# Windowed attention inside an F32 two-mixer layer: values held stationary, turned probabilities moving, and identity products at the start

## The chip, the core and the metric

The kernel runs on one core of one Trainium2 chip. Its time is the device time of one execution in microseconds (us). TensorE (PE, with its weight loads PEld), VectorE (DVE), ScalarE (ACT), GpSimd (POOL) and SyncE (SP, which issues the transfers) each work through an instruction list of their own. PE reads its stationary operand into the array with a weight load and then streams the moving operand through it; products land in PSUM, which has eight banks of 128 partitions by 512 F32 values.

## What is computed

Two layers follow one another on 512 rows of 1,024 features. The first has neighbourhood attention beside a state-space mixer and a gated FFN. The second, in which most of the change lies, is windowed attention with 16 query heads, 4 key/value heads of 64 features, a bias by relative position and one sink logit per head, and then a SwiGLU FFN.

```python
h = rmsnorm(x, mix_norm_pre) * (1.0 + sc1) + sh1
q, k, v = split(h @ w_qkv)                       # 16, 4, 4 heads of 64
# blocks of 128 queries see the block before, their own and the one behind
logits = q k^T * 64**-0.5 + bias[bucket(rel)]    # masked to |rel| <= 128
p = softmax(concat([logits, sink]))[..., :-1]
out = (p @ v).reshape(S, 16 * 64) @ w_o
x = x + g1 * rmsnorm(out, mix_norm_post)
```

## The kernel before

Weights arrive by DMA in raw F32 chunks (`wr`); ACT rounds a chunk to F32R (`wh`, L152) and DVE takes the rest (`wl`, L153), so that a product is three F32R products: high by high, high by low, low by high (`mm3`, L89 to L91). Activations are kept in the same two parts (`hh`, `hl`), with features on partitions.

The kernel is written as a program of tiles. Which instruction stands where on an engine is settled when the program is built; while it runs, each engine keeps to its list and waits for what an instruction needs. Buffers come from rings (`slots`, some with one or two buffers), and PSUM banks are handed out by roles (`psum(...)`); in the heads there are two banks for the wide products, three for scores (`PS`), two for transposes (`PT`) and one for the attention output (`PO`).

In the attention of mixer 2, `wide(...)` makes ten tiles of queries and keys, [128 features x 512 rows] each, with 24 products of 512 columns a tile. From the fourth tile on, two heads (a pair) run beside the next tile's products, so that six pairs lie beside tiles and the last two pairs (heads 12 to 15) behind them. `head(h)` takes four query blocks n. Each block has w = 256 or 384 keys, and for each:

1. two score products of w columns (L1048, L1049) into a PSUM bank;
2. DVE adds the bias and takes the row minimum (L1051, with a read of the accumulator behind it), ACT takes the exponential and the row sums (L1053);
3. PE transposes the 128x128 squares of the probabilities (L1056), two or three of them;
4. a copy brings them to SBUF, on DVE for odd blocks (L1059) and on ACT for even ones (L1061);
5. PE multiplies with the turned probabilities as the stationary operand and 64 columns of `v` moving, in F32 (L1064). There are 10 such products a head, and each is two entries in the trace: 320 entries for 16 heads.

Behind the four blocks come the sink's exponential (L1065), the sum, the reciprocal (L1066, L1067) and the scaling into `on` (L1068), with rows on partitions. `turn_o(a)` (L1073 to L1081) transposes eight finished heads back to features on partitions, in 16 transposes with a high part on ACT and a low part on DVE for each of four row blocks: once beside the last heads (for heads 0 to 7), once behind head 15 (for heads 8 to 15). The output projection then runs through `nat_out` (L825, L829) with `oT` as its stationary operand.

At the start, x is loaded, normalised on DVE (L307) and transposed on PE (L338); a row of modulation values is made by products with 32 columns of `cs32` (`gemv2`, L318) and brought to columns (`columns`, copy L324, transposes L326, L327 to L332); `features` (L340 to L342) makes `hh` and `hl`, which the first products (L89) need.

Of the kernel before, what the change touches and what calls it, by code (L numbers as in the profile page):

```python
# [11 lines left out]
F32 = mybir.dt.float32  # L12
# [26 lines left out]
def tile_hybrid_then_windowed_gqa(ctx, tc, A, out, dbg=None):  # L39
# [152 lines left out]
    make_identity(nc, ident)  # L192
    onesr = CT(128, F32R, base="one")
# [806 lines left out]
    Q, VV, BI, PS_ = slots(ap_, "q", 16), slots(ap_, "v", 2), slots(ap_, "bi", 2), slots(ap_, "sc", 3)  # L1000
    PP = slots(ap_, "pp", 3)
# [8 lines left out]
    on = [ap_.tile([128, 4, 512], F32, tag=f"on{a}", name=f"on{a}") for a in range(2)]  # L1010
# [20 lines left out]
    po2 = []  # L1031

    def head(h):
        kvh = h // 4
        bt = BI(n=384)
        nc.sync.dma_start(out=bt, in_=A["bias2"][h])
        if h % 2 == 0:
            po2.append(PO())
        po, st = po2[-1][:, 256 * (h % 2):256 * (h % 2) + 256], SS(n=20)
        for n in range(4):  # L1040
            j0, j1 = max(0, n - 1), min(4, n + 2)
            nk = j1 - j0
            w = 128 * nk
# [6 lines left out]
            sc = PS_(n=384)  # L1050
            V.tensor_tensor_reduce(sc[:, :w], s[:, :w], bt[:, b0:b0 + w], -1.0, nsink[:, h:h + 1],  # L1051
                                   ALU.add, ALU.min, st[:, n:n + 1])
            act(sc[:, :w], sc[:, :w], AF.Exp, scale=-1.0, bias=st[:, n:n + 1], accum_out=st[:, 4 + n:5 + n])  # L1053
            pt = PT()
# [10 lines left out]
        act(st[:, 8:12], st[:, 0:4], AF.Exp, bias=sk[:, h:h + 1])  # L1065
        V.tensor_add(st[:, 12:16], st[:, 4:8], st[:, 8:12])  # L1066
        V.reciprocal(st[:, 16:20], st[:, 12:16])  # L1067
        V.tensor_tensor(on[h // 8][:, :, 64 * (h % 8):64 * (h % 8) + 64], hd(po, 4),  # L1068
                        st[:, 16:20, None].to_broadcast([128, 4, 64]), op=ALU.mult)

    oT = {}

    def turn_o(a):  # L1073
        for tb in range(4):
            p = PT()
            for f in range(4):
                tr(p[:, 128 * f:128 * f + 128], on[a][:, tb, 128 * f:128 * f + 128], ident)
            hi, lo = Q(F32R), Q(F32R)
            act(hi, p, AF.Copy)
            V.tensor_sub(lo, p, hi)  # L1080
            oT[tb, a] = hi, lo  # L1081

    def use_and_attend(i, p):
# [3 lines left out]
        if i == 3:  # L1087
            ws = [load_w(Wq, 4 * a, 4, [(1280, 256)]) for a in range(2)]
            for t2 in range(2):
# [6 lines left out]
                t = VV()  # L1096
                V.tensor_copy(t, pv)
                vv.extend([t[:, 0:256], t[:, 256:512]])
# [4 lines left out]
        if i == 9:  # L1103
            turn_o(0)
# [169 lines left out]
```

## Time and profile before

| | |
|---|---|
| time, three runs | 1347.13, 1351.51, 1354.16 us (median 1351.51) |
| profiled execution | 1350.22 us, span 1348.4 us, mean granted TensorE clock 0.995 |
| busy, share of the span | PE 97%, PEld 81%, DVE 59%, ACT 43%, POOL 7% |
| chain that ended last | PE 79%, DVE 10%, DMA 4%, ACT 3%, POOL 2% |
| L1064, values times probabilities | 320 entries, PE busy 43.1 us, PEld busy 41.3 us |

The busy shares are means over stages with different limits, so that the stages have to be read one by one. In a window's row the figures are its bounds, its length, the busy time of PE, PEld, DVE, ACT and POOL with the number of instructions, the granted clock (1.00 is 2.4 GHz), the DMA engines' share and GB/s. In a timeline's row they are the start, the duration, the line and the operation; starts that follow one another closer than the durations tell what an instruction costs, since neighbours overlap. In a row of lines they are the number of instructions, their busy time, the mean duration in ns and the engine's idle time ahead of them with what ended it.

### The profile page before, as it was taken

Reading aid. Unit: us, or ns where it says so; the run is one execution under the profiler, and the core shown is the slowest. Engines: PE = TensorE matmul, PEld = TensorE weight load, DVE = VectorE, ACT = ScalarE, POOL = GpSimd, SP = SyncE. Lnnn points to the kernel's source line nnn. Section 1 sums busy time; section 2 is a strip of 40 time slices with the busy share of each in tenths; the row PEclk is TensorE's granted clock in tenths of the full one; section 3 lists DMA queues with packets and bytes.
Section 4 is the critical chain, followed back from the end, with each engine's and each line's share of the span. In section 5 each row is a group of like instructions: output and inputs, shape, how many; then the busy total and the mean of one; then the engine's idle time right before and its main releaser. Section 6 shows DMA issues by size and latency. Waiting matters only on the chain.

```text
span 1348.4 us, 18115 instructions
## 1 busy us (share of the span) xinstructions
PE 1302.4 (97%) x6927; PEld 1092.6 (81%) x6927; DVE 790.4 (59%) x1443; ACT 581.3 (43%) x1040; POOL 93.0 (7%) x101
## 2 busy tenths in 40 slices
PE   6999999998999999999999999999999999999997
PEld 3687778997879888888788798888798888888886
DVE  5786996666685766675953666666553222325323
ACT  2546446765555333333433555565552222224221
POOL 0013560000000000000000310000000000000000
PEclk9999999999999999999999999999999999999999
DMA  8763131043553654665654112212133332223321
GB/s 284 262 204 109 47 103 55 22 130 124 195 196 109 219 170 158 218 213 168 232 168 143 61 60 80 62 57 63 57 95 94 98 104 96 94 94 96 106 79 63
DMA packets 53238, 168.14 MB, mean 125 GB/s; under 512 B 6048, under 2 KB 11424, under 8 KB 53152
## 3 DMA queue, kind: packets, MB, share of 16 engines
q1 hardware_dynamic: 53152, 166.99, 38.3%
q8 instruction: 55, 0.90, 0.3%
q14 instruction: 31, 0.25, 0.1%
HBM read 164.87 MB, written 2.10 MB: 124 GB/s over the span
## 4 chain that ended last, share of the span: by engine, by line
PE 79%; DVE 10%; DMA 4%; ACT 3%; POOL 2%; issue 2%; SPq 0%; POOLq 0%; DVEq 0%; ACTq 0%
PE bank L825 19%; PE bank L89 16%; PE bank L90 16%; PE bank L91 15%; PE bank L1064 3%; PE bank L765 2%; DMA ada<-in_ada_w 2%; PE bank L1056 1%; DVE acc L226 1%; PE bank L759 1%; DVE wl L153 1%; PE bank L1048 1%; POOL sm L207 1%; PE bank L1049 1%; DMA wr<-in_w_in_tiles 1%
## 5 line engine op out<-in xcount | busy, mean ns | idle before, releaser
L90 PE MATMUL bank<-hl,wh 128*128 128x512 f32 (+1 forms) x1040 | 389.0, 374 | 2.1 <-DVE hl L917 1.5
L89 PE MATMUL bank<-hh,wh 128*128 128x512 f32 (+1 forms) x1040 | 388.5, 376 | 0.8 <-DVE b L383 0.7
L91 PE MATMUL bank<-hh,wl 128*128 128x512 f32 (+1 forms) x1040 | 388.8, 374 | 0.0
L152 ACT ACTIVATE wh<-wr 128x1024 fp32r<-128x1024 f32 x173 | 182.1, 1059 | 393.1 <-PE bank L90 286.7
L153 DVE TENSOR_TENSOR wl<-wr,wh 128x1024 fp32r<-128x1024 f32 x173 | 212.2, 1228 | 196.2 <-ACT wh L152 196.0
L90 PEld LDWEIGHTS bank<-hl,wh 128*128 128x128 f32 x1040 | 197.2, 190 | 34.8 <-DVE hl L917 2.9
L89 PEld LDWEIGHTS bank<-hh,wh 128*128 128x128 f32 x1040 | 196.4, 190 | 34.1 <-DVE b L383 1.0
L91 PEld LDWEIGHTS bank<-hh,wl 128*128 128x128 f32 x1040 | 197.1, 190 | 31.4
L825 PE MATMUL bank<-wh,act 128*128 128x512 f32 x544 | 146.2, 389 | 0.0
L825 PEld LDWEIGHTS bank<-wh,act 128*128 128x128 f32 x544 | 102.1, 188 | 21.5 <-issue 0.3
L226 DVE SCALAR_TENSOR_TENSOR acc<-ada,cs,acc 128x1024 f32<-128x1024 f32 x70 | 91.0, 1299 | 22.0 <-DMA ada<-in_ada_w 21.7
L972 DVE TENSOR_TENSOR act<-bank,act 128x512 f32<-128x512 f32 x44 | 30.4, 690 | 92.6 <-PE bank L91 92.5
L825 PE MATMUL bank<-wl,act 128*128 128x512 f32 x272 | 84.0, 389 | 0.0
L207 POOL TENSOR_TENSOR sm<-sm,mh 128x1 f32<-128x1 f32 x28 | 17.3, 618 | 657.6 <-DVE sm L206 657.6
L825 PEld LDWEIGHTS bank<-wl,act 128*128 128x128 f32 x272 | 51.0, 188 | 10.6
L825 PE MATMUL bank<-act,act 128*128 128x512 f32 x240 | 56.8, 397 | 0.0
L825 PEld LDWEIGHTS bank<-act,act 128*128 128x128 f32 x240 | 46.0, 193 | 9.7
L1064 PEld LDWEIGHTS bank<-v,pp 128*128 128x128 f32 x320 | 41.3, 191 | 5.5 <-ACT pp L1061 2.3
L1064 PE MATMUL bank<-v,pp 128*128 128x64 f32 x320 | 43.1, 271 | 0.1
L982 DVE TENSOR_TENSOR act<-act,act 128x512 fp32r<-128x512 f32 x44 | 29.5, 686 | 20.7 <-PE bank L825 20.0
L1053 ACT ACTIVATE sc<-sc,ss 128x256 f32<-128x256 f32 (+1 forms) x64 | 35.6, 557 | 12.8 <-DVE ss L1051 9.0
L1051 DVE CUSTOM_DVE_ANT_0 sc<-bank,bi,nsink 128x256 f32<-128x256 f32 (+1 forms) x64 | 33.7, 543 | 10.0 <-PE bank L1049 8.2
(324 smaller groups left out, 1885.9 us busy)
## 6 DMA issues: line engine op xcount, KB each, us to landing
ada<-in_ada_w SPq DMA_DIRECT2D x80, 512.0 KB, 4.4
wr<-in_ffn_w_up_tiles SPq DMA_DIRECT2D x44, 512.0 KB, 4.4
wr<-in_ffn_w_in_tiles SPq DMA_DIRECT2D x44, 512.0 KB, 3.6
wr<-in_ffn_w_down SPq DMA_DIRECT2D x22, 512.0 KB, 4.5
wr<-in_ffn_w_out SPq DMA_DIRECT2D x22, 512.0 KB, 3.4
wr<-in_w_in_tiles SPq DMA_DIRECT2D x19, 512.0 KB, 4.4
wr<-in_att_w_qkv_tiles SPq DMA_DIRECT2D x10, 512.0 KB, 3.7
ada<-in_ada SPq DMA_DIRECT2D x8, 512.0 KB, 5.2
```

Of the source, the lines that this page charges most:

```text
L89: mm(o, lh, rh, start=start, stop=False)
L90: mm(o, lh, rl, start=False, stop=False)
L91: mm(o, ll, rh, start=False, stop=stop)
L152: act(hi[:, :n], raw[:, :n], AF.Copy)
L153: V.tensor_sub(lo[:, :n], raw[:, :n], hi[:, :n])
L207: GP.tensor_tensor(ms[:, 1:2], ms[:, 0:1], mhalf, op=ALU.pow)
L226: V.scalar_tensor_tensor(acc, raw, csil[:, ci + k:ci + k + 1], acc, op0=ALU.mult, op1=ALU.add)
L825: mm(ps[tb][a], l, r[a], start=start and l is lh and r is w[0], stop=stop and l is ll)
L972: V.tensor_mul(actT[ft], p, actT[ft])
L1051: V.tensor_tensor_reduce(sc[:, :w], s[:, :w], bt[:, b0:b0 + w], -1.0, nsink[:, h:h + 1], ALU.add, ALU.min, st[:, n:n + 1])
L1053: act(sc[:, :w], sc[:, :w], AF.Exp, scale=-1.0, bias=st[:, n:n + 1], accum_out=st[:, 4 + n:5 + n])
L1064: mm(o, P[:, 128 * i:128 * i + 128], vv[j0 + i][:, 64 * kvh:64 * kvh + 64], start=i == 0, stop=i == nk - 1)
```

## The change

Two parts of the kernel are touched.

In the attention, operands are exchanged: `v` (now kept as a high and a low half beside one another, 128 columns for each kv head) is the stationary operand, and the turned probabilities move through it with 256 or 384 columns. For that they are kept in two F32R parts, `ph` (ACT) and `pl` (DVE), one pair of tiles for a head. A head has eight products, all into the one `PO` bank, with the product of the high half of `v` on one half of the partitions and that of the low half on the other; ACT copies one half (L1086) and DVE adds the other (L1087). Sums and reciprocals are taken apart: the reciprocals of a pair are spread over 64 columns each (L1094), transposed (L1097), and multiplied on (L1098). The pair's output is then already turned, so `turn_o` goes; its two parts (L1100, L1101) are the `oT` of one k. The score buffers are a ring of seven in place of three. In the program's text the scores of all four blocks, with what DVE and ACT do to them, now come ahead of the first transpose.

At the start, eight F32 products of the identity with a broadcast column of itself (512 columns) go into a bank that is free; nothing reads them.

```diff
+    idle = PO()
+    for _ in range(8):
+        mm(idle, ident, ident[:, 0:1].to_broadcast([128, 512]), start=True, stop=True)
...
-    Q, VV, BI, PS_ = slots(ap_, "q", 16), slots(ap_, "v", 2), slots(ap_, "bi", 2), slots(ap_, "sc", 3)
-    PP = slots(ap_, "pp", 3)
+    Q, VV, BI = slots(ap_, "q", 16), slots(ap_, "v", 2), slots(ap_, "bi", 2)
+    sc_ring = itertools.cycle([XN] * 4 + [XT] * 3)
...
+    op, sums, RS, RX = [], [], slots(ap_, "rs", 2), slots(ap_, "rx", 1)
     def head(h):
...
+            scs.append(sc)
+        act(st[:, 8:12], st[:, 0:4], AF.Exp, bias=sk[:, h:h + 1])
+        V.tensor_add(rs[:, 4 * s2:4 * s2 + 4], st[:, 4:8], st[:, 8:12])
+
+        ph, pl = (ap_.tile([128, 4, 512], F32R, tag=f"on{a}", name=nm("p")).rearrange("p a b -> p (a b)")
+                  for a in range(2))
+        for n, (j0, j1) in enumerate(spans):
+            nk, sc = j1 - j0, scs[n]
             pt = PT()
             for i in range(nk):
                 tr(pt[:, 128 * i:128 * i + 128], sc[:, 128 * i:128 * i + 128], ident)
-            P = PP(n=384)
-            if n % 2:
-                V.tensor_copy(P[:, :w], pt[:, :w])
-            else:
-                act(P[:, :w], pt[:, :w], AF.Copy)
-            o = po[:, 64 * n:64 * n + 64]
-            for i in range(nk):
-                mm(o, P[:, 128 * i:128 * i + 128], vv[j0 + i][:, 64 * kvh:64 * kvh + 64], start=i == 0, stop=i == nk - 1)
...
+            at = 256 * j0 + 128 * n + 128
+            hi, lo = (t[:, at:at + 256 * nk].rearrange("p (k n) -> p k n", k=nk)[:, :, 0:128] for t in (ph, pl))
+            src = pt[:, :128 * nk].rearrange("p (k n) -> p k n", k=nk)
+            act(hi, src, AF.Copy)
+            V.tensor_sub(lo, src, hi)
+        po = PO()
+        for j in range(4):
+            n0, n1 = max(0, j - 1), min(4, j + 2)
+            a = 384 * j + 128 * (n0 - j + 1)
+            for part in (ph, pl):
+                mm(po[:, 128 * n0:128 * n1], vv[j][:, 128 * kvh:128 * kvh + 128], part[:, a:a + 128 * (n1 - n0)],
+                   start=j == 0 and part is ph, stop=j == 3 and part is pl, skip_group_check=True)
...
+        act(o[own, :], po[other, :], AF.Copy)
+        V.tensor_add(o[own, :], po[own, :], o[own, :])
+        if s2:
+
+            V.reciprocal(rs, rs)
+            pr = PT()
+            rx = RX()
+            for s in range(2):
+                V.tensor_copy(rx.rearrange("p (n s d) -> p n s d", n=4, s=2)[:, :, s, :],
+                              rs[:, 4 * s:4 * s + 4, None].to_broadcast([128, 4, 64]))
+            for n in range(4):
+                tr(pr[:, 128 * n:128 * n + 128], rx[:, 128 * n:128 * n + 128], ident)
+            V.tensor_mul(o, o, pr)
+            hi, lo = Q(F32R), Q(F32R)
+            act(hi, o, AF.Copy)
+            V.tensor_sub(lo, o, hi)
+            oT[h // 2] = hi, lo
...
-                t = VV()
-                V.tensor_copy(t, pv)
...
+                act(tv[:, :, 0, :], hd(pv, 8), AF.Copy)
+                V.tensor_sub(tv[:, :, 1, :], hd(pv, 8), tv[:, :, 0, :])
...
-        if i == 9:
-            turn_o(0)
...
-    turn_o(1)
     def lhs_o(tb, k):
-        hi, lo = oT[tb, k // 4]
-        c = slice(128 * (k % 4), 128 * (k % 4) + 128)
+        hi, lo = oT[k]
+        c = slice(128 * tb, 128 * tb + 128)
```

On PE the change shows most beside a wide tile. Before, this stands there in one pair (`pp` holds turned probabilities, `sc` the ones not yet turned, `q` queries and keys, `hh`, `hl`, `wh`, `wl` the wide tile):

```order
L1064 MATMUL bank_7801<-v_7090,pp_7812 128x64 x2
L1056 MATMUL bank_7837<-id_107,sc_7834 128x128 x3
L89 MATMUL bank_7932<-hh_6457,wh_7928 128x512
L90 MATMUL bank_7932<-hl_6458,wh_7928 128x512
L91 MATMUL bank_7932<-hh_6457,wl_7929 128x512
L89 MATMUL bank_7932<-hh_6457,wh_7928 128x512
L1064 MATMUL bank_7801<-v_7090,pp_7826 128x64 x2
L1064 MATMUL bank_7801<-v_7141,pp_7826 128x64
L1064 MATMUL bank_7801<-v_7090,pp_7841 128x64
L1064 MATMUL bank_7801<-v_7141,pp_7841 128x64 x2
L1056 MATMUL bank_7852<-id_107,sc_7849 128x128 x2
```

After the change, in the same stage (`p` holds one part of the turned probabilities, `xn` and `xt` take the place of `sc`, `rx` holds the spread reciprocals):

```order
L1080 MATMUL bank_7814<-p_7791,v_7097 128x256
L1080 MATMUL bank_7814<-p_7790,v_7097 128x384
L1053 MATMUL bank_7898<-q_6960,q_7689 128x256
L1054 MATMUL bank_7898<-q_6963,q_7689 128x256
L91 MATMUL bank_8026<-hh_6466,wl_8023 128x512
L89 MATMUL bank_8026<-hh_6466,wh_8022 128x512
L1080 MATMUL bank_7814<-p_7791,v_7097 128x384
L1080 MATMUL bank_7814<-p_7790,v_7149 128x384
L1080 MATMUL bank_7814<-p_7791,v_7149 128x384
L1080 MATMUL bank_7814<-p_7790,v_7149 128x256
L1080 MATMUL bank_7814<-p_7791,v_7149 128x256
L1097 MATMUL bank_7826<-id_107,rx_7827 128x128 x4
```

Single products of 64 columns, each with a weight load of its own from `pp`, have become products of 256 or 384 columns on two weights of `v`, and four more transposes of `rx` stand in a pair.

On DVE, before, in the same pair as above, one head's four score blocks with the work between them:

```order
L1051 ISA sc_7806,ss_7802<-bank_7803,bi_7799,nsink_6741 128x256
L1051 ISA ss_7802 128x1
L1051 ISA sc_7819,ss_7802<-bank_7816,bi_7799,nsink_6741 128x384
L1051 ISA ss_7802 128x1
L1051 ISA sc_7834,ss_7802<-bank_7831,bi_7799,nsink_6741 128x384
L1051 ISA ss_7802 128x1
L1027 SCALAR_TENSOR_TENSOR q_7793<-bank_7768,q_7793 64x512
L1051 ISA sc_7849,ss_7802<-bank_7846,bi_7799,nsink_6741 128x256
L1051 ISA ss_7802 128x1
L153 TENSOR_TENSOR wl_8479<-wr_8090,wh_8478 128x1024
L1027 SCALAR_TENSOR_TENSOR q_7796<-bank_7768,q_7796 64x512
L1059 COPY pp_7826<-bank_7822 128x384
```

On DVE after the change, across the end of one head and the start of the next pair's first:

```order
L1074 TENSOR_TENSOR p_7791<-bank_7803,p_7790 128x3x128
L1074 TENSOR_TENSOR p_7791<-bank_7809,p_7790 128x2x128
L1094 COPY rx_7827<-rs_7698 128x4x64 x2
L1056 ISA xt_7889,ss_7878<-bank_7886,bi_7876,nsink_6750 128x384
L1056 ISA ss_7878 128x1
L1056 ISA xt_7895,ss_7878<-bank_7892,bi_7876,nsink_6750 128x384
L1056 ISA ss_7878 128x1
L1087 TENSOR_TENSOR tm_7758<-bank_7814,tm_7758 64x512
L1056 ISA xn_7901,ss_7878<-bank_7898,bi_7876,nsink_6750 128x256
L1056 ISA ss_7878 128x1
L1098 TENSOR_TENSOR tm_7758<-tm_7758,bank_7826 128x512
L1074 TENSOR_TENSOR p_7907<-bank_7908,p_7906 128x2x128
```

The copies of `pp` on every second block are gone; a subtraction that reads the bank and ACT's part (L1074) stands there for every block, and the two copies into `rx`, the addition, the multiplication and the low part of the output (which follows this piece) have come in.

On PE at the start, before, the transposes of x (`b`) stand first, and half of them ahead of the products on the modulation weights (`ada`, `n`):

```order
L338 MATMUL bank_179<-id_107,b_77 128x128
L338 MATMUL bank_179<-id_107,b_81 128x128
L338 MATMUL bank_229<-id_107,b_77 128x128
L338 MATMUL bank_229<-id_107,b_81 128x128
L318 MATMUL bank_158<-ada_93,sel_120 32x256 x4
L318 MATMUL bank_158<-n_95,sel_120 32x256 x2
L318 MATMUL bank_158<-n_97,sel_120 32x256 x2
L338 MATMUL bank_179<-id_107,b_85 128x128
L338 MATMUL bank_179<-id_107,b_89 128x128
L338 MATMUL bank_229<-id_107,b_85 128x128
L338 MATMUL bank_229<-id_107,b_89 128x128
L326 MATMUL bank_158<-id_107,t_167 128x128 x2
```

After the change:

```order
L196 MATMUL bank_112<-id_107 128x512 x8
L322 MATMUL bank_167<-ada_93,sel_129 32x256 x4
L322 MATMUL bank_167<-n_95,sel_129 32x256 x2
L322 MATMUL bank_167<-n_97,sel_129 32x256 x2
L342 MATMUL bank_188<-id_107,b_77 128x128
L342 MATMUL bank_188<-id_107,b_81 128x128
L342 MATMUL bank_188<-id_107,b_85 128x128
L342 MATMUL bank_188<-id_107,b_89 128x128
L322 MATMUL bank_209<-ada_101,sel_129 32x256
L330 MATMUL bank_167<-id_107,t_176 128x128 x2
```

The identity products stand ahead of everything, and the first set of modulation products ahead of the first transposes of x.

## Rows read from the trace of the kernel before

**Rows 1.** Windows: six pairs beside tiles; the sixth alone; heads 12 to 15.

```profile
816.60:905.69 89.09, 89.09 (x604) 78.19 (x602) 58.78 (x174) 54.66 (x150) 0.00 (x0) 1.00 0.23 69
890.88:905.69 14.81, 14.81 (x102) 13.00 (x100) 9.72 (x29) 9.06 (x26) 0.00 (x0) 1.00 0.20 64
905.69:936.20 30.51, 29.70 (x214) 25.66 (x213) 21.63 (x64) 20.75 (x56) 0.00 (x0) 1.00 0.16 49
```

**Rows 2.** Timeline of PE inside the sixth pair.

```profile
895.91 0.48 PE L89 MATMUL bank<-hh,wh 128*128 128x512 f32 x1
896.22 0.40 PE L90 MATMUL bank<-hl,wh 128*128 128x512 f32 x1
896.46 0.40 PE L91 MATMUL bank<-hh,wl 128*128 128x512 f32 x1
...
896.92 1.45 PE L1064 MATMUL bank<-v,pp 128*128 128x64 f32 x12
898.21 0.39 PE L1056 MATMUL bank<-id,sc 128*128 128x128 f32 x2
898.35 0.36 PE L1048 MATMUL bank<-q,q 128*128 128x256 f32 x1
```

**Rows 3.** Timeline of PE, products of 256 columns in F32R.

```profile
784.54 0.28 PE L89 MATMUL bank<-hh,wh 128*128 128x256 f32 x1
784.66 0.28 PE L90 MATMUL bank<-hl,wh 128*128 128x256 f32 x1
```

**Rows 4.** Lines of DVE in the sixth pair, forms apart.

```profile
L1051 DVE CUSTOM_DVE_ANT_0 sc<-bank,bi,nsink 128x384 f32<-128x384 f32 x4 | 2.3, 606 | 0.0
L1051 DVE CUSTOM_DVE_ANT_0 sc<-bank,bi,nsink 128x256 f32<-128x256 f32 x4 | 1.9, 481 | 1.5 <-PE bank L1049 1.5
L1027 DVE SCALAR_TENSOR_TENSOR q<-bank,q 64x512 fp32r<-64x512 f32 x2 | 1.4, 690 | 0.1
L153 DVE TENSOR_TENSOR wl<-wr,wh 128x1024 fp32r<-128x1024 f32 x1 | 1.2, 1221 | 0.0
L1059 DVE COPY pp<-bank 128x384 f32<-128x384 f32 x2 | 1.1, 558 | 0.0
L1059 DVE COPY pp<-bank 128x256 f32<-128x256 f32 x2 | 0.8, 425 | 2.4 <-ACT ss L1065 1.6 <-PE bank L1056 0.8
```

**Rows 5.** Lines of ACT in the sixth pair, forms apart.

```profile
L1026 ACT ACTIVATE q<-bank 64x512 fp32r<-64x512 f32 x2 | 1.2, 583 | 0.0
...
L1061 ACT ACTIVATE pp<-bank 128x384 f32<-128x384 f32 x2 | 1.0, 492 | 0.6 <-PE bank L1056 0.6
```

**Rows 6.** Timeline of PE at the start.

```profile
10.59 1.30 PE L338 MATMUL bank<-id,b 128*128 128x128 f32 x4 [10.59 <-DVE b L307]
...
14.16 1.29 PE L338 MATMUL bank<-id,b 128*128 128x128 f32 x4 [0.37 <-DVE b L307]
...
22.54 0.63 PE L91 MATMUL bank<-hh,wl 128*128 128x512 f32 x1
22.96 0.53 PE L90 MATMUL bank<-hl,wh 128*128 128x512 f32 x1
```

**Rows 7.** Timeline of PE, one F32 product of 256 columns (two entries).

```profile
139.60 0.59 PE L630 MATMUL bank<-n,b 128*128 128x256 f32 x2
140.03 0.38 PE L613 MATMUL bank<-b,b 128*128 128x128 f32 x2
```

**Rows 8.** Timeline of DVE at the start.

```profile
13.62 1.67 DVE L307 TENSOR_SCALAR b<-b,ss 128x512 f32<-128x512 f32 x4 [0.82 <-POOL ss L304]
...
16.94 1.22 DVE L153 TENSOR_TENSOR wl<-wr,wh 128x1024 fp32r<-128x1024 f32 x1
18.08 0.42 DVE L341 CAST hh<-t 128x512 fp32r<-128x512 f32 x1
```

**Rows 9.** Timeline of PE behind an idle time at the start of mixer 2.

```profile
780.84 1.86 PE L909 MATMUL bank<-id,xn 128*128 128x128 f32 x8 [2.70 <-DVE xn L902]
```

**Rows 10.** Window on the 3.36 us behind that idle time.

```profile
780.84:784.20 3.36, 3.36 (x16) 3.36 (x17) 2.23 (x5) 2.68 (x9) 1.62 (x2) 0.52 0.01 2
```

More of the change, by code (lines that the diff above doesn't have):

```diff
@@ L1009, in tile_hybrid_then_windowed_gqa @@
     V.tensor_scalar(nsink, sk, -1.0, None, op0=ALU.mult)
-    on = [ap_.tile([128, 4, 512], F32, tag=f"on{a}", name=f"on{a}") for a in range(2)]
     vv = []
@@ L1029, in use_qkv @@
                 qs[2 * (i - 2) + s] = t
-    po2 = []
+    op, sums, RS, RX = [], [], slots(ap_, "rs", 2), slots(ap_, "rx", 1)
     def head(h):
-        kvh = h // 4
+        kvh, s2 = h // 4, h % 2
         bt = BI(n=384)
         nc.sync.dma_start(out=bt, in_=A["bias2"][h])
[L1037 to L1043, printed above, removed]
+        st, scs = SS(n=20), []
+        if s2 == 0:
+            sums.append(RS(n=8))
+        rs = sums[-1]
+        spans = [(max(0, n - 1), min(4, n + 2)) for n in range(4)]
+        for n, (j0, j1) in enumerate(spans):
+            w = 128 * (j1 - j0)
             b0 = 128 * (j0 - n + 1)
@@ L1049, in head @@
             mm(s[:, :w], qs[h][:, qa], kl[kvh][:, ka], start=False, stop=True)
-            sc = PS_(n=384)
+            sc = next(sc_ring)(n=384)
             V.tensor_tensor_reduce(sc[:, :w], s[:, :w], bt[:, b0:b0 + w], -1.0, nsink[:, h:h + 1],
@@ L1053, in head @@
             act(sc[:, :w], sc[:, :w], AF.Exp, scale=-1.0, bias=st[:, n:n + 1], accum_out=st[:, 4 + n:5 + n])
+            scs.append(sc)
[3 more added lines that the diff above has]
+                  for a in range(2))
+        for n, (j0, j1) in enumerate(spans):
+            nk, sc = j1 - j0, scs[n]
             pt = PT()
@@ L1056, in head @@
                 tr(pt[:, 128 * i:128 * i + 128], sc[:, 128 * i:128 * i + 128], ident)
-            P = PP(n=384)
-            if n % 2:
-                V.tensor_copy(P[:, :w], pt[:, :w])
-            else:
-                act(P[:, :w], pt[:, :w], AF.Copy)
-            o = po[:, 64 * n:64 * n + 64]
-            for i in range(nk):
-                mm(o, P[:, 128 * i:128 * i + 128], vv[j0 + i][:, 64 * kvh:64 * kvh + 64], start=i == 0, stop=i == nk - 1)
-        act(st[:, 8:12], st[:, 0:4], AF.Exp, bias=sk[:, h:h + 1])
@@ L1066, in head @@
[L1066 to L1069, printed above, removed]
-    oT = {}
[L1073 to L1081, printed above, removed]
+            at = 256 * j0 + 128 * n + 128
@@ new lines, in head @@
+        own, other = slice(64 * s2, 64 * s2 + 64), slice(64 - 64 * s2, 128 - 64 * s2)
+        if s2 == 0:
+            op.append(TM())
+        o = op[-1]
+        act(o[own, :], po[other, :], AF.Copy)
[14 more added lines that the diff above has]
+            oT[h // 2] = hi, lo
@@ L1095, in use_and_attend @@
                             ws[k // 4][1][:, k % 4, :], k == 0, k == 7)
-                t = VV()
-                V.tensor_copy(t, pv)
-                vv.extend([t[:, 0:256], t[:, 256:512]])
+                t = VV(F32R, 1024)
+                tv = t.rearrange("p (g s d) -> p g s d", g=8, s=2)
+                act(tv[:, :, 0, :], hd(pv, 8), AF.Copy)
+                V.tensor_sub(tv[:, :, 1, :], hd(pv, 8), tv[:, :, 0, :])
+                vv.extend([t[:, 0:512], t[:, 512:1024]])
             psum(pa=(6, 4), s=(1, 2, 3), pt=(7, 0), po=(5,))
```

## The prediction

> **What bounds the kernel now.** I read the page first: PE is busy for 97% of the span and has most of the chain that ended last. That says where to look, not what an edit is worth, so I next read the windows of the heads [rows 1]. In the six pairs beside wide tiles (816.60 to 905.69) PE is busy for all of the 89.09 us, so the stage is PE's, and a pair takes 89.09 / 6 = 14.85 us. In the sixth alone DVE is busy for 9.72 us and ACT for 9.06 us of 14.81. The other engines have some 5 us of room a pair, and what leaves PE there is gained until one of them takes over. Between heads 12 and 15 PE has a little idle time (29.70 of 30.51).
>
> What PE's pair is made of comes from starts in its timeline [rows 2, 3]:
>
> - 24 products of 512 columns, 0.24 apart (896.22 to 896.46): 5.7 us.
> - 16 score products. 256 columns are 0.12 apart [rows 3]; for 384 I take the middle between that and 0.24, 0.18. 8 x 0.12 + 8 x 0.18 = 2.4 us.
> - 20 transposes, 0.07 each (898.21 to 898.35 for two): 1.4 us.
> - 40 entries of L1064, twelve of them from 896.92 to 898.21: 0.1075 each, 4.3 us.
> - The rest, 14.8 - 13.8 = 1.0 us, is the turn from F32 entries back to F32R: the first product behind transposes takes 0.31 (895.91 to 896.22) in place of 0.24, and there are 10 to 13 such turns.
>
> **The pair, on PE.** The 40 entries go (-4.3 us). Eight products a head come, all F32R: half of 256, half of 384 columns, 2 x (4 x 0.12 + 4 x 0.18) = +2.4 us. Four transposes of `rx` come: +0.3. Some four turns to F32R go, since the new products are F32R themselves: -0.3. PE needs 14.8 - 1.9 = 12.9 us a pair.
>
> **The pair, on DVE.** Removed are four copies of `pp` (2 x 0.558 + 2 x 0.425 = 1.97) and two scalings (L1068, 128x256 out of a bank, priced as the 0.425 copy: 0.85) [rows 4]. Added, from the nearest rows:
>
> - Eight subtractions out of a bank, 384 or 256 columns, at the copies' durations: 4 x 0.558 + 4 x 0.425 = 3.93.
> - Two additions of 64x512 out of a bank, as L1027: 1.38.
> - The multiplication and the low part of the output, 128x512, 0.69 each by the same row: 1.38.
> - Two copies into `rx`, 128x256 from SBUF to SBUF. From a bank that is 0.425 [rows 4]; a cast inside SBUF takes 0.42 for twice the columns [rows 8], so that half of it, 0.21, is the lower bound. I take 0.3: 0.6. One reciprocal fewer takes 0.1 away.
>
> The balance is 3.93 + 1.38 + 1.38 + 0.6 - 0.1 - 1.97 - 0.85 = +4.4, so that DVE needs 9.72 + 4.4 = 14.1 us at these durations. They overstate it where instructions lie against one another: L153 starts at 16.94, lasts 1.22, and the next starts at 18.08 [rows 8], 0.08 before its end. For some 14 of the 36 instructions, which now touch their neighbours, that is -1.1: 13.0 us if DVE never waits.
>
> A page of the Trainium skill bears on the price of the copies: "VectorE: DVE Perf Modes" (Mode 2×_2P — use both read ports for one tensor) says that a one-source F32 operation inside SBUF runs at twice the rate, and one that reads PSUM does not. Rows 8 against rows 4 agree in kind; by the rule the copies would stand at the lower bound, and the pair 0.2 us lower. It also means that the eight subtractions, which read a bank, can't become cheap.
>
> **The pair, on ACT.** Four copies go and eight come; at 0.49 each [rows 5], which is too much for the 256 ones, +2.0 at most. Two copies of 64x512 (L1086) and one high part of 512 columns (L1100) at 0.583 [rows 5] add 1.75. ACT needs 9.06 + 3.7 = 12.8 us at most.
>
> So DVE, not PE, has the longest list: 13.0 without waits, 14.1 at full durations, against PE's 12.9. Waits come on top, because the subtraction stands in a chain: PE turns a block, ACT makes the high part (0.49), only then DVE can subtract (0.56). With two `PT` banks, a block that waits for ACT holds up DVE's list, where the next head's scores stand behind the subtractions, as the order shows. That chain is about 1.3 us per block and the list is long enough to cover most of it. I take 14.0: about 1 us of waiting in the pair on top of 13.0, near the sum at full durations. Bounds: 13.0 (nothing waits) and 15.3 (a wait of 0.28 us at each of eight subtractions on top of 13.0). **Six pairs: 6 x (14.0 - 14.85) = -5.1 us, from -11 to +2.7.**
>
> `ph` and `pl` have one buffer each, and `PO` one bank. The next head's transposed parts wait until this head's eight products are read, 1.2 us behind its last subtraction; the bank is free after one copy and one addition, another 1.3 us. In a half pair of 7 us both fit; I cost them at nothing, and if PE came to these products late they would be the 15.3 above.
>
> **Heads 12 to 15 and the output projection.** PE loses 2 x 1.9 us and `turn_o`'s 32 transposes (2.2 us): 29.70 - 6.0 = 23.7 of work. DVE has 21.63 [rows 1], gains 2 x 4.4, and loses `turn_o`'s eight low parts (5.5): 24.9. But the order puts the end of the pair before (four subtractions, copies, addition, multiplication, low part: 4.5 us) behind the first scores of head 12, inside this stretch: 29.4, and 1 to 2 us of the chain's waits: some 31 against 30.51. On the other side a pair's output is now ready as one k of the projection, so that PE can put products of it into DVE's gaps. I take 0, from -3 to +3.
>
> **The values.** `v` is copied by ACT and subtracted by DVE instead of copied by DVE alone, twice 0.7 us on ACT. PE goes on to scores and tiles that don't need `v`; nothing, and 1 us if the first product of values came sooner than that.
>
> **The start.** PE is idle until 10.59 [rows 6]. The identity is there at about 1.3 us, and eight F32 products, two entries of 512 columns each, start. An entry of 256 columns takes (140.03 - 139.60) / 2 = 0.215 [rows 7]; 512 columns are 0.43 at the higher clock level and 0.86 at the lower: 16 entries take 6.9 to 13.8 us, so they end between 8.2 and 15.1. At the upper end they would push PE's first real work back, but the modulation products, now first in its list, have their input only at about 12.2 and the second half of x is normalised from 13.62 on [rows 8]; that bounds the harm at 2 us. What they can give is speed: the early products stand 0.42 apart (22.54 to 22.96), nearly twice the 0.24 of rows 2, so the 3.2 us from 19.79 to 22.96 could shrink by half, -1.6. Against that stands what PE did after 2.70 us of idle time [rows 9]: in the 3.36 us behind it the granted clock was 0.52, the lower level [rows 10]. Between the last identity product and 19 us PE has gaps and small work as before. DVE's list also has the 1.22 us L153 earlier there, ahead of the modulation's last steps. I take -0.5, from -2 to +2.
>
> The Trainium skill's page "TensorE: Matmul & The Clock Gate" (Part 1, HAM oscillation — how this bites in real kernels) speaks against this part: where PE waits between its bursts, the clock falls back each time, so that warmth has to be kept and not only made. Rows 9 and 10 agree. By it, what the identity products give is lost in the gaps before the first real products, the start is 0 and the sum 0.5 us higher.
>
> **Sum.** Of the execution's own 1350.2 us (span 1348.4): -5.1 + 0 - 0.5 = -5.6, about 1345. The execution lies 1.3 us under the median of the runs shown, well inside their spread.
>
> **Rivals.**
> - *Full relief* (0.24): DVE's list packs, the chain is covered, pairs fall to 13.1 and the tail gives 2 to 3. 6 x -1.75 - 2.5 - 0.5 = -13.5: 1337. For it: DVE and ACT each have long lists of independent work. Against it: three engines, all at 12.8 to 13.1, must then mesh.
> - *Traded bound, no gain* (0.23): pairs of 14.6 to 15.0, as now, because DVE's durations hold at 14.1 and the waits are 0.5 to 0.9; the start gives nothing: 1349 to 1351. For it: DVE idles now partly behind PE, and it will idle behind ACT.
> - *Slower* (0.13): the subtraction's wait for ACT's part. It decides from 14.85 - 13.0 = 1.85 us of DVE waiting in a pair on; at 3 us a pair takes 16.0, +6.9, and the tail +2: 1359; at 2.3 with the tail +3 and the start's -0.5, 1355. For it: a single buffer behind a single bank; against it: PE's list has nine wide products a head to fill in.
> - *The start alone decides* (within the others): the clock stays up, -1.6 to -2, or the first work is late, +2.
>
> My forecast, 13.6 to 14.4 a pair, has 0.40, and by itself gives 1340 to 1348. **Range:** the lower end takes in most of full relief, 1336, the upper the milder slower case, 1355. About 0.5% (6.8 us, under 1344.8 or over 1358.3) is what a measurement of this kernel can tell from no change. The forecast lies at that edge: half of it (0.20) and full relief give 0.44 faster; the other half, the traded bound and the mildest of the slower cases (0.03) give 0.46; slower by more than that has 0.10.
>
> **What would show it.** In the pairs: PE's busy time near 12.9 with idle time ended by ACT or DVE, DVE busy 13 or more of 14, L1074 waiting for ACT's L1073. In the tail: DVE near 30 us to the last L1101. At the start: the identity products' length, the spacing of the products at 19 to 23 us. It is wrong if PE stays at 100% in the pairs (then its products cost more than their columns) or if L1080 is found waiting long for L1074.

## The result

The changed kernel takes 1336.78 us (median of 4 runs, 1332.34 to 1339.02), the kernel before, with one more run beside it, 1349.32 (1346.32 to 1354.16): ratio 0.9894, 95% interval 0.9875 to 0.9913. In a second session (experiment 8 below) it was 0.9906 (0.9881 to 0.9930). The change makes the kernel some 12 us, about 1%, faster. I had forecast 1345. The time lies in the range, near its lower end, but the gain is more than twice the forecast: 5.6 us were forecast, and 14.2 lie between the two profiled executions.

The windows of the profile after come first: the first pair of heads, the second, a steady one, all six beside wide tiles, and heads 12 to 15 with the output projection. The columns are those of [rows 1].

```profile
810.88:823.07 12.19, 12.17 (x71) 10.15 (x69) 10.38 (x31) 10.71 (x29) 0.00 (x0) 1.00 0.38 120
823.07:835.44 12.37, 12.37 (x76) 10.59 (x76) 11.55 (x29) 9.33 (x26) 0.00 (x0) 1.00 0.18 58
849.22:862.84 13.62, 13.56 (x82) 11.54 (x80) 12.66 (x37) 12.03 (x37) 0.00 (x0) 1.00 0.11 31
810.88:890.27 79.39, 79.19 (x465) 66.80 (x464) 72.50 (x202) 67.46 (x187) 0.00 (x0) 1.00 0.19 57
890.27:961.70 71.43, 67.62 (x339) 55.40 (x337) 51.75 (x122) 44.03 (x114) 2.74 (x5) 0.98 0.25 80
```

Rows 1 start with a neighbour's record at 816.60; the first score before is at 816.72, and the same two stretches are:

```profile
816.72:832.56 15.84, 15.84 (x106) 13.77 (x105) 10.07 (x29) 9.40 (x25) 0.00 (x0) 1.00 0.31 93
816.72:905.69 88.97, 88.97 (x603) 78.07 (x601) 58.68 (x174) 54.66 (x150) 0.00 (x0) 1.00 0.23 69
905.69:975.92 70.23, 69.00 (x393) 57.51 (x391) 42.43 (x101) 40.29 (x102) 2.74 (x5) 1.00 0.20 59
```

A steady pair takes 13.6 us in place of 14.8 (13.7 on average over four, from 835.44 to 890.27), and PE is busy for all but 0.06 us of this one. The six pairs gain 88.97 - 79.39 = 9.6 us, of which the first alone gives 15.84 - 12.19 = 3.65. Behind them there are 70.23 us before and 71.43 after; a clock at 0.98 costs the second some of that (it is 70.15 in the same kernel's second profile, at 1.00). So the gain of the attention lies where wide tiles run beside it.

DVE's lines in the steady pair answer to [rows 4]:

```profile
L1074 DVE TENSOR_TENSOR p<-bank,p 128x384 fp32r<-128x384 f32 x4 | 2.2, 556 | 0.2 <-ACT p L1073 0.2
L1087 DVE TENSOR_TENSOR tm<-bank,tm 64x512 f32<-64x512 f32 x3 | 2.0, 682 | 0.2 <-ACT tm L1086 0.2
L1074 DVE TENSOR_TENSOR p<-bank,p 128x256 fp32r<-128x256 f32 x4 | 1.7, 413 | 0.0
...
L1101 DVE TENSOR_TENSOR q<-tm,q 128x512 fp32r<-128x512 f32 x1 | 0.7, 693 | 0.4 <-ACT q L1100 0.4
L1098 DVE TENSOR_TENSOR tm<-tm,bank 128x512 f32<-128x512 f32 x1 | 0.7, 683 | 0.0
...
L1094 DVE COPY rx<-rs 128x256 f32<-128x256 f32 x2 | 0.6, 286 | 0.0
```

The prices held: the subtractions take 0.556 and 0.413 us (I had put 0.558 and 0.425), the additions 0.682 (0.69), the multiplication 0.683 and the low part 0.693 (0.69), a copy into `rx` 0.286 (0.3). DVE is busy for 12.66 us, where the sum gave 13.0 without waits, and idle for 0.96 us in the pair; the waits for ACT's high part (L1073) are 0.2 us of it.

PE's timeline in the same pair answers to [rows 2]:

```profile
849.99 0.49 PE L1069 MATMUL bank<-id,xn 128*128 128x128 f32 x3
850.53 0.39 PE L1080 MATMUL bank<-p,v 128*128 128x256 f32 x1
850.75 0.35 PE L1054 MATMUL bank<-q,q 128*128 128x384 f32 x1
...
852.64 0.39 PE L89 MATMUL bank<-hh,wh 128*128 128x512 f32 x1
852.87 0.92 PE L1080 MATMUL bank<-p,v 128*128 128x384 f32 x5
853.63 0.60 PE L1097 MATMUL bank<-id,rx 128*128 128x128 f32 x4
854.06 0.38 PE L1069 MATMUL bank<-id,xn 128*128 128x128 f32 x2
854.20 0.42 PE L1053 MATMUL bank<-q,q 128*128 128x384 f32 x1
```

Five values products stand 0.15 apart on average (852.87 to 853.63), and two transposes take 0.14 (854.06 to 854.20), as priced; the first product of values behind transposes takes 0.22 in place of 0.12 (850.53 to 850.75), which is the turn from F32. The three transposes at 849.99 take 0.54 up to that product, and that is a wait: ACT is still making a high part (L1073) until 850.47, and the weight load of the values product stands idle for it.

```profile
850.00 0.47 ACT L1073 ACTIVATE p<-bank 128x384 fp32r<-128x384 f32 x1
850.53 0.19 PEld L1080 LDWEIGHTS bank<-p,v 128*128 128x128 f32 x1 [0.29 <-ACT p L1073]
```

The duration of the transposes, 0.49, covers all but 0.05 us of this wait, so that PE counts as busy in it. A busy share near 100% therefore doesn't say that PE waits for nothing. Over the four steady pairs the weight loads wait 4.5 us in all; the three largest sums are these (total, times, longest):

```profile
PEld bank L1080 <- ACT p L1073: 2.3, 8, 0.4
PEld bank L1069 <- DVE p L1074: 0.6, 2, 0.4
PEld bank L1069 <- ACT xn L1058: 0.5, 1, 0.5
```

An estimate of PE's list without waits: give every product in these pairs the median distance to the next start that its kind shows there (by its line's work and columns, and by whether F32 or F32R stands on either side of it). That sums to 51.7 us, 12.9 a pair, where 54.83, 13.7 a pair, were measured. Some 0.8 us a pair is then waiting, nearly all of it hidden in PE's busy time.

At the start, where [rows 6] stood:

```profile
1.36 9.94 PE L196 MATMUL bank<-id 128*128 128x512 f32 x16 [1.36 <-POOL id masks.py:199]
11.62 0.64 PE L322 MATMUL bank<-ada,sel 128*32 128x256 f32 x8 [0.33 <-DMA ada<-in_ada]
...
21.25 1.17 PE L89 MATMUL bank<-hh,wh 128*128 128x512 f32 x4
22.26 0.39 PE L90 MATMUL bank<-hl,wh 128*128 128x512 f32 x1
22.49 0.40 PE L91 MATMUL bank<-hh,wl 128*128 128x512 f32 x1
```

The identity products take 9.9 us and end at 11.3, inside the bounds of 8.2 and 15.1. The first product of a wide tile is later than before (21.25 against 19.79), but from 22.26 on its neighbours are 0.23 apart. The identity products themselves start 0.85 us apart up to 6.64 and 0.43 apart from 7.25 on. Between 17.2 and 20.6 the granted clock is at the lower of its two levels (1.2 GHz):

```profile
17.20:20.60 3.40, 3.29 (x20) 1.69 (x21) 1.34 (x6) 1.34 (x2) 0.00 (x0) 0.51 0.87 343
```

### The profile page after: what moved, and what is told of

It reads as the page before. It is cut to its first block, busy times and chain, and to the rows that moved or that the text cites. A ratio compares the mean times of both kernels' runs of the same rounds, so it can differ in the third digit from the quotient of the medians.

```text
span 1334.2 us, 17792 instructions
## 1 busy us (share of the span) xinstructions
PE 1296.5 (97%) x6751; PEld 1082.7 (81%) x6751; DVE 813.3 (61%) x1491; ACT 599.1 (45%) x1090; POOL 94.9 (7%) x101
## 4 chain that ended last, share of the span: by engine, by line
PE 77%; DVE 10%; DMA 5%; ACT 4%; issue 2%; POOL 2%; SPq 0%; POOLq 0%; DVEq 0%; ACTq 0%
PE bank L829 18%; PE bank L90 16%; PE bank L89 16%; PE bank L91 16%; PE bank L769 2%; PE bank L1080 1%; DVE wl L153 1%; DMA ada<-in_ada_w 1%; PE bank L1069 1%; DMA wr<-in_w_in 1%; PE bank L763 1%; DVE acc L230 1%; POOL sm L211 1%; ACT wh L152 1%; DVE hl L921 1%
## 5 line engine op out<-in xcount | busy, mean ns | idle before, releaser
L971 ACT ACTIVATE act<-act 128x512 f32<-128x512 f32 x22 | 13.9, 633 | 57.4 <-DVE act L970 57.4
L916 ACT ACTIVATE tm<-bank,mod 128x128 f32<-128x128 f32 x96 | 35.8, 458 | 7.2 <-PE bank L913 4.2
L985 ACT ACTIVATE act<-act 128x512 fp32r<-128x512 f32 x44 | 26.7, 623 | 24.1 <-DVE act L986 21.5
L895 POOL TENSOR_TENSOR xn<-x,ada 128x512 f32<-128x512 f32 x8 | 10.5, 1313 | 354.8 <-DVE x L869 350.8
```

The costliest lines, as they stand in the source:

```text
L916: act(full[:, 128 * i:128 * i + 128], p[:, 128 * i:128 * i + 128], AF.Identity, scale=mod[:, 8 + k:9 + k], bias=mod[:, k:k + 1])
L985: act(hi, actT[k], AF.Copy)
```

## Experiments

Below, *the stretch* is the time from head 0's first score to the first product behind the output projection, read from the timeline: 816.72 to 975.92 before, 159.2 us; 810.88 to 961.70 after, 150.8.

**1. The exchange alone.** The changed kernel without the identity products:

```diff
-    idle = PO()
-    for _ in range(8):
-        mm(idle, ident, ident[:, 0:1].to_broadcast([128, 512]), start=True, stop=True)
```

> The exchange of operands without the identity products; the start is that of the kernel before. Read from the two traces, the whole change lies 5.7 us ahead of the kernel before at the first score of head 0 and 14.2 us ahead at the end of the output projection. If the two parts add up, this kernel gains 8 to 9 us (ratio 0.9935 to 0.994) and its first 800 us run as before. If the earlier start also shapes the attention (other transfers, another clock), it gains under 6 us or over 11.

Measured: 1339.69 us (6 runs), ratio 0.9934 (0.9915 to 0.9953), by which it gains 8.9 us (8.3 between the medians). The first score of head 0 is at 816.35, as before, and the stretch is 149.55 us, 9.65 less.

```profile
816.35:895.72 79.37, 79.15 (x466) 66.66 (x464) 72.49 (x202) 67.48 (x187) 0.00 (x0) 1.00 0.19 58
895.72:965.90 70.18, 66.55 (x338) 53.64 (x336) 51.66 (x122) 43.90 (x113) 2.74 (x5) 1.00 0.25 81
```

So the attention is worth some 9 us by itself, 9.65 in this stretch, and the whole of it lies in the six pairs; the 70.2 us behind them are what they were.

**2. The identity products alone**, on the kernel before (the three lines above added).

> The identity products without the exchange. If the parts add up: 5 to 6 us faster (ratio 0.9955 to 0.9965), with nearly all of it won by 120 us. By the term of the prediction: 0.5 us, no difference.

Measured: 1346.26 us (12 runs), ratio 0.9989 (0.9977 to 1.0001): 1.5 us, with nothing just inside the interval. The 5.8 us that the profiles before and after show ahead of head 0's first score are not there. The term of the prediction, -0.5 us with bounds of -2 and +2, is not contradicted.

**3 and 4. Order and products apart.** With the products, the build puts the first instructions of four engines in another order. Experiment 3 has that order without the products, experiment 4 the products in the old order. Both fix the order with edges that only say what is issued first:

```diff
     with tile.TileContext(nc) as tc:
         tile_hybrid_then_windowed_gqa(tc, aps, out)
+        insts = {i.name: i for i in nc.cur_bb.bb.instructions}
+        for queue in ([...], [...], [...], [...]):
+            names = [f"I-{k}" for k in queue]
+            for p, q in zip(names, names[1:]):
+                if p in insts and q in insts:
+                    tc.add_manual_dep(insts[q], p, mybir.DependencyInfo(
+                        mybir.DependencyClass.NoSync, mybir.DependencyReason.DATA), reason="order")
```

> No identity products and the old attention, but the first 292 instructions of PE, 159 of DVE, 53 of ACT and 64 transfers stand in the order that they have in the kernel with the products. Theory of the order (the products gain because the build's planner, seeing PE taken, lines up transfers and work otherwise): 3 to 5 us faster (ratio 0.9965 to 0.998). Theory of the clock (what counts is that PE is busy before the first real products): within 1 us of the kernel before.

> The eight identity products are there, but everything else stands in the order of the kernel before. Theory of the order: within 1 us of the kernel before, or slower. Theory of the clock: 3 to 5 us faster (ratio 0.9965 to 0.998), with the products from 20 to 23 us 0.23 apart and no stretch at the lower clock at 112 us.

Measured: order alone 1347.01 us (12 runs), ratio 0.9992 (0.9979 to 1.0006); products in the old order 1347.26 (12 runs), 0.9990 (0.9976 to 1.0005). The ratios give 1.1 and 1.3 us, and 3 us lies at the end of both intervals: neither theory's 3 to 5 us came, and the two are not told apart. The profile of experiment 4 shows what the products do to the spacing where nothing else moves:

```profile
1.36 9.05 PE L196 MATMUL bank<-id 128*128 128x512 f32 x16 [1.36 <-POOL id masks.py:199]
...
19.56 0.50 PE L90 MATMUL bank<-hl,wh 128*128 128x512 f32 x1
19.90 0.39 PE L91 MATMUL bank<-hh,wl 128*128 128x512 f32 x1
20.13 0.40 PE L90 MATMUL bank<-hl,wh 128*128 128x512 f32 x1
```

The first products of the tile are 0.23 apart from 19.90 on, in place of 0.42 [rows 6], and no stretch at the lower clock follows at 17 us or at 112 us. Why it follows at 17 us in the changed kernel and not here isn't shown: ahead of it, from 14.0 to 17.2, PE is busy for 1.55 of 3.20 us there and for 1.64 here. Experiment 3 has the closer spacing as well, without any identity product:

```profile
20.62 0.39 PE L90 MATMUL bank<-hl,wh 128*128 128x512 f32 x1
20.85 0.39 PE L91 MATMUL bank<-hh,wl 128*128 128x512 f32 x1
```

So either part brings the early products to 0.23 in its profile, and that is worth no more than the ratios above. The granted clock of the kernel before reads 1.00 there too (20.60 to 24.00), where its products are 0.42 apart; that the clock is behind the spacing is read from the halving alone.

**5. DVE relieved.** The changed kernel without the low part of the probabilities (missing from the output; PE multiplies the high part twice):

```diff
             act(hi, src, AF.Copy)
-            V.tensor_sub(lo, src, hi)
...
-            for part in (ph, pl):
+            for rep, part in enumerate((ph, ph)):
...
```

> The changed kernel without DVE's eight subtractions a pair; the second product of each two takes the high part again, so that PE has the same products, and the low part of the probabilities is missing from the output. DVE loses 3.3 to 3.9 us a pair. Theory of DVE (its list and its waits for ACT set the 13.7 us of a steady pair): pairs of 12.9 to 13.1 us, PE's own sum. Theory of PE (PE has no more than 0.1 us of idle time a pair, so its list is the bound, only longer than I summed): 13.5 to 13.7 us as before.

One run; a steady pair, the stretch in its two parts, and the first pair:

```profile
857.56:871.41 13.85, 13.75 (x81) 11.10 (x80) 10.38 (x29) 11.73 (x33) 0.00 (x0) 1.00 0.22 67
816.34:899.14 82.80, 82.24 (x483) 67.01 (x481) 60.04 (x167) 70.34 (x192) 0.00 (x0) 1.00 0.24 74
899.14:962.30 63.16, 62.77 (x321) 51.00 (x319) 39.01 (x93) 41.64 (x108) 2.75 (x5) 1.00 0.21 65
816.34:830.59 14.25, 14.25 (x87) 12.21 (x86) 8.88 (x26) 11.84 (x32) 0.00 (x0) 1.00 0.32 103
```

Pairs stay at 13.85 us though DVE is busy for only 10.4 of them, so that DVE's list is not what sets a steady pair. It doesn't follow that PE's list is: the estimate of PE without waits is 12.9 here too, and over the four steady pairs (843.51 to 899.14) transposes wait for ACT's high part for 3.1 us:

```profile
PEld bank L1069 <- ACT p L1073: 3.1, 8, 0.7
```

The surprise is at both ends. Heads 12 to 15 with the output projection take 63.2 us in place of 70.2, and the six pairs 82.80 in place of the 79.30 of experiment 8. The build orders this kernel so that every pair is done when the next one's first score starts: PE has then done all 20 transposes of the scores, all 16 values products and all four transposes of `rx` at each boundary. The first pair takes 14.25 us, in the changed kernel 12.19. So half of the 7.0 us is work that no longer moves behind the pairs; the other 3.5 are won in the whole stretch (145.96 against 149.45). Total 1336.63 us (one run); the start of that run was some 3 us later than in experiment 8.

**6. PE relieved.** One score product in place of two (the low part of the keys is missing from the scores):

```diff
-            mm(s[:, :w], qs[h][:, qa], kk[kvh][:, ka], start=True, stop=False)
-            mm(s[:, :w], qs[h][:, qa], kl[kvh][:, ka], start=False, stop=True)
+            mm(s[:, :w], qs[h][:, qa], kk[kvh][:, ka], start=True, stop=True)
```

> The changed kernel without the second score product of each block (the low part of the keys is missing from the scores): PE loses 8 products, 1.2 us a pair by their starts; DVE and ACT keep all their work. Theory of DVE: pairs stay at 13.4 to 13.7 us. Theory of PE: 12.4 to 12.6 us.

One run; the two pairs from 860.82 to 887.77, which hold just the work of two pairs, and the stretch behind head 12's first score:

```profile
860.82:887.77 26.95, 26.58 (x146) 20.21 (x144) 24.15 (x73) 23.89 (x65) 0.00 (x0) 1.00 0.11 31
887.77:965.25 77.48, 70.67 (x337) 56.06 (x336) 55.78 (x128) 47.26 (x121) 2.75 (x5) 0.96 0.24 76
```

With 1.2 us less to do, PE wins only 0.2: 26.95 / 2 = 13.5 us a pair, which is what the theory of DVE said, where experiment 5 had come out near the theory of PE. Neither list alone sets the pair. The estimate without waits is now 11.8 us a pair, so that PE waits for some 1.7 while it counts as busy for 13.3. In these two pairs the weight loads of values products wait 1.7 us for ACT's high part, and other weight loads wait for DVE:

```profile
PEld bank L1079 <- ACT p L1072: 1.7, 6, 0.4
PEld bank L1068 <- DVE p L1073: 1.1, 4, 0.4
```

With PE or DVE relieved, the handovers from PE to ACT and DVE and back keep a pair at 13.5 to 13.9 us. No run relieves ACT, so that its share is not measured. The stretch as a whole got longer (809.05 to 965.25, 156.2 us): PE now waits, and twice its granted clock falls to the lower level for 6.8 us (from 831.5 and from 899.8; the second row's mean is 0.96). That costs up to 6.8 us, about what the stretch is longer than in experiment 8.

**7. DVE loaded.** The copies into `rx` done twice:

```diff
-            for s in range(2):
+            for s in (0, 1, 0, 1):
                 V.tensor_copy(rx.rearrange("p (n s d) -> p n s d", n=4, s=2)[:, :, s, :],
```

> The changed kernel with the two copies into the spread reciprocals done twice: DVE has 0.5 us more a pair (0.285 a copy), nothing else changes. Theory of DVE: pairs of 14.1 to 14.3 us. Theory of PE: 13.6 to 13.8 us.

One run: three steady pairs take 41.42 us, 13.8 each, 0.1 longer than in experiment 8. That lies in the range of the theory of PE and shows again that DVE's list is not the bound there. The stretch is 152.8 us, 3.3 longer, and the added copies sum to 8 x 0.57 = 4.6. How much of the 3.3 is DVE's extra work isn't shown, because the build also ordered this kernel otherwise: only 2 of the sixth pair's 24 wide products lie in that pair (878.77 to 890.27, 11.5 us), the other 22 behind head 12's first score.

```profile
837.35:878.77 41.42, 41.41 (x241) 34.61 (x240) 38.60 (x115) 36.00 (x99) 0.00 (x0) 1.00 0.10 30
```

**8. The changed kernel again**, without an edit.

> The changed kernel itself, timed in more rounds. If the two parts only add up, the ratio is 0.9934 x 0.9989 = 0.992 (10 to 11 us faster), and the 14 us between the two profiles hold some us of chance at the start; if the parts help each other, it stays at 0.989 to 0.990.

Measured: 1336.24 us (6 runs, 1334.57 to 1339.59), ratio 0.9906 (0.9881 to 0.9930). The product of experiments 1 and 2, 0.992, lies inside, and so does 0.9894: that the parts add up and that they help each other by a little are not told apart. The stretch is 149.45 us (813.65 to 963.10).

**9. Seven score buffers in the kernel before.**

```diff
+    sc_ring = itertools.cycle([XN] * 4 + [XT] * 3)
...
-            sc = PS_(n=384)
+            sc = next(sc_ring)(n=384)
```

> The kernel before with the ring of seven score buffers in place of three, nothing else. Theory of PE (the six pairs were PE's before, so that scores made earlier only move PE's work): the stretch from the first score of head 0 to the first product behind the output projection stays at 159.2 us, within 1. Theory of the buffers (the deeper ring alone lets the first pairs run ahead): 155 to 157 us.

One run: the stretch is 160.5 us (819.64 to 980.12), 1.3 longer. That is a little outside what the theory of PE allowed, and on the side away from the theory of the buffers: the ring alone gives nothing (its steady pairs take 15.15 us against 14.81).

**10. Four score buffers in the changed kernel.**

```diff
-    sc_ring = itertools.cycle([XN] * 4 + [XT] * 3)
+    sc_ring = itertools.cycle([XN] * 4)
```

> The changed kernel with four score buffers in place of seven. Theory of work carried over (the first two pairs take 12.2 and 12.4 us because their later steps move on to the next pairs, and the last heads give it back): the first two pairs get longer by 0.5 to 1.5 us each, heads 12 to 15 with the output projection get shorter by as much, the stretch stays at 149.5 within 1 us. Theory of the buffers (running ahead is itself a gain): the stretch gets 2 to 4 us longer.

One run, and a miss for the first theory's detail. The first two pairs take 12.35 and 11.8 us (809.06, 821.41, 833.17), not more, the last two 14.2, and the stretch is 152.1 us. That is 1.3 more than in the changed kernel's own profile, which has a stretch of lower clock at the same place (from 903.5 here, from 901.3 there). That the first pairs leave work behind does not hang on the number of score buffers.

**11. Two of DVE's jobs on GpSimd.**

```diff
-                V.tensor_copy(rx.rearrange("p (n s d) -> p n s d", n=4, s=2)[:, :, s, :],
+                GP.tensor_copy(rx.rearrange("p (n s d) -> p n s d", n=4, s=2)[:, :, s, :],
...
-            V.tensor_sub(lo, o, hi)
+            GP.tensor_tensor(lo, o, hi, op=ALU.subtract)
```

> The changed kernel with the two copies into the spread reciprocals (L1094) and the low part of the output (L1101) on GpSimd, which is idle there: DVE loses 2 x 0.285 + 0.69 = 1.26 us a pair. If DVE is what the last heads wait for (PE idles 3.6 us in the 69.9 us behind head 12's first score), that stretch gets 1.5 to 3 us shorter, and the steady pairs, which PE fills, stay at 13.6 to 13.8: 2 to 3 us faster than the changed kernel (ratio about 0.988). If GpSimd is slow enough to stand in the chain (reciprocals, transposes, output), the last pair ends later: no gain or 1 to 3 us of loss.

Measured: 1334.64 us (5 runs, 1332.17 to 1336.05), ratio 0.9892 (0.9872 to 0.9911). The stretch is 147.0 us, 2.5 shorter than in experiment 8: behind head 12's first score 66.75 in place of 70.15 us, with PE idle for 0.9 us there in place of 3.6, while the six pairs take 0.9 longer. Three transposes and one values product more lie ahead of head 12's first score, which is some 0.5 us of the shift between the two parts.

```profile
811.82:892.05 80.23, 79.80 (x469) 67.21 (x468) 72.29 (x194) 69.19 (x189) 10.27 (x16) 1.00 0.24 76
892.05:958.80 66.75, 65.87 (x335) 52.67 (x334) 45.61 (x106) 43.17 (x112) 8.81 (x14) 1.00 0.19 62
```

In experiment 8, PE's waits in the stretch are nearly all for DVE (3.4 of 3.6 us), and they lie behind head 12's first score; the two largest are:

```profile
PE bank L1069 <- DVE p L1074: 1.3, 2, 0.7
PE bank L829 <- DVE ss L1056: 1.1, 1, 1.1
```

With the two jobs on GpSimd, 0.4 us of the first are left, and the second is gone. It is the fastest kernel of the study by median and by the trace; by the two ratios alone it isn't told apart from the changed kernel.

## Why the prediction was wrong

**What was right.** The list of PE and the prices on DVE. The 40 entries of L1064 cost 4.3 us a pair; eight products a head take 2.9 in their place (2.4 were priced, and part of the rest is waiting), and that is where the gain comes from. PE without waits needs 12.9 us a pair by the estimate above, as forecast. The value copies, the single buffers of `ph` and `pl` and the one `PO` bank cost nothing that shows. The copies into `rx` take 0.286 us for 256 columns inside SBUF, where a copy out of a bank took 0.425 for as many [rows 4]. The Trainium skill's page "VectorE: DVE Perf Modes" (Mode 2×_2P — use both read ports for one tensor) says that a one-source F32 operation inside SBUF runs at twice the rate. The trace agrees in kind, though the time is not half.

**The step that failed first: "So DVE, not PE, has the longest list ... I take 14.0."** A steady pair takes 13.7 us (54.83 / 4), and DVE's list does not set it: with 2.3 us less of DVE's work a pair takes 13.85 (experiment 5), with 0.57 more 13.8 (experiment 7). DVE's 12.66 us of work lie under my lower bound of 13.0, and it waits for L1073 only 0.2 us in the pair. What I had on the wrong engine is the wait. I put 1 us of waiting for ACT's high part on top of DVE's list; the runs show it on PE, whose values products need that part too: 12.9 us of list and some 0.8 of waits. That "PE stays at 100% in the pairs" was my sign of being wrong, and it came, but the reason that I gave with it, that the products cost more than their columns, is not what the starts show. Cost: 0.3 us a pair, 1.7 of the 4.6 us by which six pairs at 14.0 (84.0 us) miss the measured 79.39.

**The step that failed more: the six pairs as six steady pairs, and work carried over charged without a credit.** I read from the order that the end of a pair stands behind the next pair's first scores, and charged 4.5 us of it to heads 12 to 15. But what one pair hands on, the first pair has not done. Counted in the second profile (experiment 8): when head 2's first score starts, PE has done 15 of 20 transposes, 9 of 16 values products and none of the four for `rx`; at head 12's first score it is 115 of 120, 88 of 96 and 20 of 24. Before, all were done at both points. By the distances in the steady pairs (0.092 for a transpose, 0.18 for a values product, 0.109 for one of `rx`) that is 5 x 0.092 + 8 x 0.18 + 4 x 0.109 = 2.3 us of PE's work that moves from the first two pairs to the last heads. The first two pairs take 24.56 us, 2.9 less than two steady ones, and that is the rest of the 4.6. Experiment 5 is the test of it: there nothing is carried over, and the first two pairs take 27.17 us (816.34 to 843.51) against 27.8 for two of its steady ones, so that 2.2 of the 2.9 go away with the carried work. The 0 that I took for the last heads is right (70.2 before, 70.15 and 70.18 after) although they take on that work, and the six pairs give 9.6 us in place of 5.1.

**The start.** The term was -0.5, from -2 to +2; experiment 2 measures -1.5 with an interval from -3.1 to +0.1. The changed kernel's granted clock did fall ahead of its first wide products (0.51 from 17.2 to 20.6, behind a stretch in which PE was busy for 1.55 of 3.20 us). The Trainium skill's page "TensorE: Matmul & The Clock Gate" (Part 1, HAM oscillation — how this bites in real kernels) says that the clock falls back where PE waits between bursts, and this row agrees. In the old order (experiment 4) it did not fall there, with PE busy for 1.64 of 3.20 us, and the gain was no larger: 1.3 us by the ratio, with 3.2 inside the interval. What each of order and clock gives stays open: they are smaller than what 12 runs can tell.

**The sum.** -9.6 and -1.5 make -11.1, against 12.5 and 12.3 us between the medians of the two sessions. "Full relief", with 0.24, named the time, 1337, but not for its reasons: it had pairs of 13.1 and a shorter end. The range reached down to 1336 for that rival's sake, so that the time lies in it by luck. "Slower" needed 1.85 us of DVE waiting in a pair; it is idle for 0.96.

**What is shown and what is argued.** That DVE's list does not set the steady pairs is shown (experiments 5 and 7), and that PE's list alone does not either (6). That the handover through ACT does is argued from the waits of the weight loads; no run makes ACT faster. That PE waits for DVE behind the pairs is shown by its waits and by experiments 5 and 11, in one profile each. That the exchange and the products add up holds within some 3 us (1, 2, 8). That carried-over work is the larger part of what the first pairs gain beyond a steady one rests on the counts and on experiment 5, where both are gone together (DVE's subtractions are gone there too); experiment 10, meant to undo it, did not. The change also moves the scores ahead of the transposes in the text, and no run has that apart from the exchange of operands.

## What to carry to other kernels

When a stage is software-pipelined, price its first repetition, its steady ones and what comes behind apart, and book work that moves on once: what the end has to pay, the beginning has been given. When an edit brings three engines to within a microsecond of each other, expect the next relief of any one of them to show somewhere else; here DVE's gained only in the last heads, where no wide tile feeds PE. Don't read a busy share of 100% as a list without waits: look at the distances between starts and at the waits of the weight loads. And compare stretches of the trace, not ends of single executions: 5.8 of the 14.2 us between the two profiles lay ahead of the attention, and only 1.5 of them could be measured again.

## What the runs showed that I had not expected

The granted clock of the same program falls at some places in one execution and not in another. In the kernel before it did here:

```profile
111.90:115.30 3.40, 3.40 (x10) 2.63 (x9) 2.29 (x6) 2.36 (x4) 0.00 (x0) 0.51 0.72 218
```

The profiles of experiments 1, 2, 3, 5, 7, 8 and 9 have such a stretch at 108 to 113 us too, the first profile of the changed kernel and those of experiments 4, 6, 10 and 11 none; experiment 8 is the same program as the changed kernel. Half the clock for 3.4 us is at most 1.7 us of PE's work. How much of the spread of some 10 us between executions of one kernel comes from such places isn't shown.

GpSimd takes 1.30 us for the 128x512 subtraction that DVE does in 0.69, and 0.40 for the copy that DVE does in 0.286:

```profile
L1101 POOL TENSOR_TENSOR q<-tm,q 128x512 fp32r<-128x512 f32 x8 | 10.4, 1301 | 64.0 <-ACT q L1100 64.0
L1094 POOL COPY rx<-rs 128x256 f32<-128x256 f32 x16 | 5.9, 401 | 64.0 <-DVE rs L1090 56.5 <-PE bank L1069 4.5 <-PE bank L90 3.0
```

In that run's stretch it was still a gain: no wait there of PE, DVE or ACT is for one of these two jobs.
